# One key tile stacked from high and low parts, read once, with the queries in both halves; the rotation of two pairs of query tiles in the other order

## The chip, the cores and the metric

The kernel runs on one core of one Trainium2 chip. The metric is device time in microseconds (us) of one execution. TensorE (PE, with its weight loads PEld), VectorE (DVE), ScalarE (ACT) and GpSimd (POOL) compute; SyncE (SP) and ACT issue the transfers (DMAs) that are spoken of here. A file of instructions runs in order on each engine, and an instruction that waits holds up all behind it on its engine, the DMAs that the engine issues among them.

## The reference

One encoder layer on two batches with the same weights, T = 512 + 256 = 768 tokens of width D = 2048, in fp32:

```
h = rmsnorm(x);  z = h @ w_in        # columns: 1024 fourier | 1024 q | 256 k | 256 v
of = Re(fft2 over (tokens, 128 channels)) of each of 8 groups, times a 128x128 matrix each
q, k = rope(q), rope(k)              # 16 query heads, 4 key/value heads, head_dim 64
oa = softmax of q k^T / 8 within +-128 tokens, with a sink per head in the denominator, times v
x = x + concat(rmsnorm(of), rmsnorm(oa)) @ w_out
u = relu(rmsnorm(x) @ w_up);  x = x + (u*u) @ w_down;  y = rmsnorm(x)
```

## The kernel before

A value in fp32 is split into a high part, rounded to the fast fp32r format, and a low part, the remainder; a product of two such values is then three fp32r matmuls (high by high, high by low, low by high). For weights ACT makes the high part (`wh`, L69) and DVE the low part (`wl`, L70) of a `raw` tile loaded by SP (L79).

The phases are, in time: the values and the first products of the Fourier group (L268, L391), the in-projection together with the Fourier stages and the rotary step, the attention together with the out-projection (L1046, L1048), the MLP up (L1193) and the MLP down (L1628).

The in-projection (`pz`, L802) runs in 20 pieces of 48 matmuls, four pieces to a *pair*, which is 256 columns as two tiles of 128. Pair 0 is the keys, pairs 1 to 4 are queries; `order` gives the group g of heads that a pair feeds (pair 1 feeds g = 2, pair 2 g = 0, pair 3 g = 1, pair 4 g = 3). At the end of a pair ACT copies PSUM into a tile `zs` (L815), one COPY for each of two column tiles and two halves of the tokens. Pairs 0 and 1 go to DRAM and are read back later by SP (`load_z`, L678). Pairs 2 and 3 keep their `zs` in one buffer that they use in turn.

The rotary step of a pair goes over three slices of 256 tokens. For each slice POOL makes two products with the sine table (`cross`, `zy`, L687), DVE multiplies by the cosine (`turned`, L694) and adds or subtracts `zy` (L696), and `parts` makes the high part `zh` on ACT (L706 for keys, L709 for queries), writes it to DRAM from ACT's queue (`put`, L704), makes the low part on DVE (L707, L710) and writes that also. The tables of sine, cosine and mask are loaded by SP in `open_attention` (L664), and DVE scales two of them (L666). `zy` and `zh` have two buffers each.

What is done beside the matmuls is hung on the pieces by `after(piece, fn)`, half pieces included; this list sets the place of cross, turned and parts, of `load_z`, `load_k` (L719) and `load_q` (L730). TensorE's order is written out throughout; the order of the other engines comes from a scheduler up to piece 18 and is written out from piece 19 on. The pool `kp` holds mask, sine, cosine, keys, `zy`, `zh`, one `zs` and the query tiles `qs`.

In the attention there are 24 units (b, g): 128 query tokens and the four heads of group g, against up to 384 keys. A score tile takes two matmuls over 128 contraction rows, which are 64 head dimensions times two parts (`qk`, L848). Before, `qs` holds the high part of the queries in partitions 0 to 63 and the low part in 64 to 127, `kdh` holds the high part of the keys twice and `kdl` the low part twice, so that `qs` by `kdl` and `qs` by `kdh` add up all four products. Four loads of 64x3072 fill `kdh` and `kdl`; two loads fill `qs` of a unit, whose buffers are two.

## Time and profile before

| | us |
|---|---|
| median of three runs (2589.88, 2593.62, 2589.92) | 2589.92 |
| the profiled execution | 2589.64 |
| its span, first to last instruction | 2587.8 |
| in-projection: piece 11 ends / piece 15 ends | 311.4 / 344.91 |
| first score matmul | 378.9 |
| TensorE's last matmul ends | 2579.9 |

The mean granted TensorE clock is 0.999 of full speed. In the rows of the profile, times are us from the start of the span; in a row of the timeline stand start, duration, engine, line and operation with output and inputs, shape, number of instructions put together, and in brackets the idle time of the engine before it with what ended it. PEld is TensorE's loading of stationary operands, SPq and ACTq are the queues from which DMAs are issued.

## The change

Three things are changed. First, the keys' high and low parts are written to one DRAM tile of 512 rows and read by one load of 128x3072 into one tile `kd`, high part in partitions 0 to 63, low part in 64 to 127. Second, `qs` of a unit becomes twice as large: the high part in both halves of the partitions and the low part in both halves, four loads for two; the score is `kd` by the low queries plus `kd` by the high queries. Third, the rotary step of pair 1 moves in the list from 16.5 to 13.5 (its load from 12 to 11), ahead of pair 3's, which stays at 15. The load of the keys is one item at 15, those of the first two units' queries move from 18 and 18.5 to 17.5 and 18. The two `zs` in `kp` get two buffers, and `zh` takes a tile of the size of the new `qs`.

```diff
-    kr_d = [dpool.tile([2 * P, T], F32, tag=f"k{c}", name=f"k{c}") for c in "hl"]
+    kr_d = dpool.tile([4 * P, T], F32, tag="k", name="k")
...
-            for name in ("kdh", "kdl"):
-                kt[name] = kp.tile([P, NKV, T], F32R, tag=name, name=name)
+            kt["kd"] = kp.tile([P, NKV, T], F32R, tag="kd", name="kd")
...
-            zt[pair] = (zo["p"] if pair in (2, 3) else kt["kp"]).tile([P, 2, T], F32, tag="zs", name="zs")
+            zt[pair] = zo["p"].tile([P, 2, T], F32, tag="zs", name="zs") if pair in (2, 3) else kt["kp"].tile([P, 2, T], F32, tag="zs", name="zs", bufs=2)
...
-            out, scale = (kr_d, None) if pair == 0 else (qr_d[order[pair]], HD ** -0.5)
-            hi = kt["kp"].tile([P, 2, 256], F32R, tag="zy" if pair == len(cols) - 1 else "qs", name="zh", bufs=2)
+            out, scale = ([kr_d[o * 2 * P : (o + 1) * 2 * P] for o in range(2)], None) if pair == 0 else (qr_d[order[pair]], HD ** -0.5)
+            if pair == len(cols) - 1:
+                hi = kt["kp"].tile([P, 2, 256], F32R, tag="zy", name="zh", bufs=2)
+            else:
+                hi = kt["kp"].tile([P, 2, 4, P], F32R, tag="qs", name="zh", bufs=2)[:, 0].rearrange("p (b h) t -> p b (h t)", b=2)
...
-        def load_k(i):
-            h = slice(i % 2 * HD, (i % 2 + 1) * HD)
-            nc.sync.dma_start(f32(kt["kdh" if i < 2 else "kdl"][h]), kr_d[i // 2][:].rearrange("(d h) t -> d h t", h=NKV))
+        def load_k():
+            nc.sync.dma_start(f32(kt["kd"][:]), kr_d[:].rearrange("(p h) t -> p h t", h=NKV))
...
-            qs = kt["kp"].tile([P, 4, P], F32R, tag="qs", name="qs", bufs=2)
+            qs = kt["kp"].tile([P, 2, 4, P], F32R, tag="qs", name="qs", bufs=2)
             state[u] = {"qs": qs}
-            for o in range(2):
-                nc.sync.dma_start(f32(qs[o * HD : (o + 1) * HD]), qr_d[g][o][:, t0].rearrange("(d h) t -> d h t", h=4))
+            for i in range(2):
+                for o in range(2):
+                    nc.sync.dma_start(f32(qs[i * HD : (i + 1) * HD, o]), qr_d[g][o][:, t0].rearrange("(d h) t -> d h t", h=4))
...
-        for pair, t, ahead in ((0, 10.5, 10), (2, 11.5, None), (3, 15, None), (1, 16.5, 12)):
+        for pair, t, ahead in ((0, 10.5, 10), (2, 11.5, None), (1, 13.5, 11), (3, 15, None)):
...
-        for i in range(4):
-            after(14.5 + i, lambda i=i: load_k(i))
+        after(15, load_k)
         for u in range(2):
-            after(18 + 0.5 * u, lambda u=u: load_q(u))
+            after(17.5 + 0.5 * u, lambda u=u: load_q(u))
...
-            for n, kd in enumerate((kdl, kdh)):
-                nc.tensor.matmul(s[:, :nk], st["qs"][:, h, :], kd[:, g, k0 * P : k0 * P + nk], start=(n == 0), stop=(n == 1))
+            for o in range(2):
+                nc.tensor.matmul(s[:, :nk], st["qs"][:, 1 - o, h, :], kd[:, g, k0 * P : k0 * P + nk], start=(o == 0), stop=(o == 1))
```

On ACT, after the third slice of pair 2, before the change (`wh_3666` and `wh_3736` are weights of pair 4; `zs_3696` is the tile of pair 3; qh0 and ql0 are the DRAM tiles of group 0):

```order
L709 ACTIVATE zh_3583<-zs_3403 128x512
L704 DMA qh0_82<-zh_3583 128x2x256
L704 DMA ql0_83<-zs_3403 128x2x256
L69 ACTIVATE wh_3666<-raw_3554 128x4x4x64
L69 ACTIVATE wh_3736<-raw_3616 128x4x4x64
L815 COPY zs_3696<-pz_3457 128x384
L815 COPY zs_3696<-pz_3458 128x384
```

The same place on ACT after the change (line numbers move by one or two; `zs_3455` is the tile of pair 1, qh2 and ql2 the DRAM tiles of group 2, `zs_3719` the tile of pair 3, `wh_3689` and `wh_3767` the former `wh_3666` and `wh_3736`):

```order
L711 ACTIVATE zh_3673<-zs_3455 128x512
L69 ACTIVATE wh_3689<-raw_3552 128x4x4x64
L706 DMA qh2_85<-zh_3673 128x2x256
L706 DMA ql2_86<-zs_3455 128x2x256
L711 ACTIVATE zh_3681<-zs_3455 128x512
L706 DMA qh2_85<-zh_3681 128x2x256
L706 DMA ql2_86<-zs_3455 128x2x256
L711 ACTIVATE zh_3725<-zs_3455 128x512
L706 DMA qh2_85<-zh_3725 128x2x256
L706 DMA ql2_86<-zs_3455 128x2x256
L69 ACTIVATE wh_3767<-raw_3614 128x4x4x64
L816 COPY zs_3719<-pz_3457 128x384
```

The parts of pair 1 now stand ahead of the COPYs of pair 3; before they came behind them and behind pair 3's own parts.

On SP, from the load of pair 0's `zs` on, before the change:

```order
L678 DMA zs_3371<-zs0_78 128x2x768
L79 DMA raw_3465<-in_w_in 128x4x256
L79 DMA raw_3554<-in_w_in 128x4x256
L719 DMA kdh_3369<-kh_80 64x3072
L678 DMA zs_3548<-zs1_79 128x2x768
L79 DMA raw_3616<-in_w_in 128x4x256
L719 DMA kdh_3369<-kh_80 64x3072
L79 DMA raw_3670<-in_w_in 128x4x256
L719 DMA kdl_3370<-kl_81 64x3072
```

And after the change:

```order
L677 DMA zs_3369<-zs0_78 128x2x768
L677 DMA zs_3455<-zs1_79 128x2x768
L79 DMA raw_3465<-in_w_in 128x4x256
L79 DMA raw_3552<-in_w_in 128x4x256
L720 DMA kd_3368<-k_80 128x3072
L79 DMA raw_3614<-in_w_in 128x4x256
L79 DMA raw_3693<-in_w_in 128x4x256
```

The load of pair 1's `zs` moved up behind that of pair 0, and one load of the keys stands where four stood among the weights.

On DVE, after the last `wl` that stands ahead of pair 1's steps, after the change:

```order
L70 TENSOR_TENSOR wl_3611<-raw_3465,wh_3610 128x4x4x64
L693 TENSOR_TENSOR zs_3455<-zs_3455,cosr_3360 128x2x256 x2
L695 TENSOR_TENSOR zs_3455<-zs_3455,zy_3640 128x256
L712 SCALAR_TENSOR_TENSOR zs_3401<-zs_3401,zh_3581 128x2x256
L695 TENSOR_TENSOR zs_3455<-zs_3455,zy_3640 128x256
L695 TENSOR_TENSOR zs_3455<-zs_3455,zy_3643 128x256 x2
L693 TENSOR_TENSOR zs_3455<-zs_3455,cosr_3360 128x2x256
L712 SCALAR_TENSOR_TENSOR zs_3455<-zs_3455,zh_3673 128x2x256
L695 TENSOR_TENSOR zs_3455<-zs_3455,zy_3686 128x256 x2
L70 TENSOR_TENSOR wl_3690<-raw_3552,wh_3689 128x4x4x64
L712 SCALAR_TENSOR_TENSOR zs_3455<-zs_3455,zh_3681 128x2x256
```

Before the change `wl_3613` (now `wl_3611`) was followed by the low part of pair 2's last slice and by three `wl`.

More of the change, by code (lines that the diff above doesn't have):

```diff
@@ L832, in hybrid_encoder @@
     pp3 = att.enter_context(tc.tile_pool(name="pp3", bufs=1, space=PSUM, reuse_waits="tile"))
-    mask, sink, kdh, kdl = (kt[c] for c in ("mask", "sink", "kdh", "kdl"))
+    mask, sink, kd = (kt[c] for c in ("mask", "sink", "kd"))
     def key_blocks(b):
```

## The prediction

> **What bounds the kernel now.** I read the page first, then the waits of TensorE (its matmul stream PE and its weight loads PEld), and then the timeline of the one stretch that the change rewrites.

> ```profile
> PE 2575.5 (100%) x13580; PEld 2358.4 (91%) x13580; DVE 1812.4 (70%) x2222; ACT 1124.0 (43%) x1574; POOL 249.6 (10%) x353
> PE 94%; DVE 2%; DMA 1%; POOL 1%; ACT 0%; issue 0%; SPq 0%; ACTq 0%; POOLq 0%; DVEq 0%
> ```

> TensorE is busy 2575.5 of the span's 2587.8 us, and the chain that ended last is 94% PE. Nothing in the change removes a matmul: each score tile still takes two of the same shape. So the change can give at most what TensorE now waits for, and it can cost whatever new wait it brings. Two lists, of PE and of its weight loads, of which I show two rows each:

> ```profile
> PE pv L391 <- ACT wh L69: 1.1, 1, 1.1
> ...
> PE pz L802 <- ACT zs L815: 0.4, 1, 0.4
> ```

> ```profile
> PEld pu L1193 <- ACT o L1211: 1.3, 7, 0.2
> PEld pz L802 <- ACT zs L815: 0.9, 2, 0.7
> ```

> Columns are total us, times, longest. The first row of each pair is the largest of its list. Only `pz L802 <- ACT zs L815` lies in the stretch that is rewritten, and it is 0.4 us on PE (the weight loads run ahead of the matmuls, so theirs of 0.9 is mostly covered). That is the whole gain on offer there. A gain of over 0.2% (5.2 us, which is about what a measurement of this kernel can tell from no change) isn't there to be had. The question is what new waits cost. The place of that one wait, on the timeline:

> ```profile
> 344.40 0.51 PE L802 MATMUL pz<-xs,wl 128*128 128x384 f32 x2
> ...
> 344.80 0.86 ACT L815 COPY zs<-pz 128x384 f32<-128x384 f32 x2 [2.10 <-PE pz L802]
> ...
> 345.33 1.17 PE L802 MATMUL pz<-xf,wh 128*128 128x384 f32 x4 [0.42 <-ACT zs L815]
> ```

> Piece 15 ends on PE at 344.91; piece 16 needs a PSUM bank that ACT's first COPY of pair 3 empties, and starts at 345.33. There is no slack here: each us by which ACT reaches that COPY later is a us on the kernel.

> **The change, part by part.**

> *Earlier tables and earlier rotation (pairs 0 and 2).* The keys' tiles take less room in the pool, so its first tiles lie elsewhere; the order's waits show the load of the mask freed by the last matmul of the second Fourier stage instead of POOL's `ssf` sum.

> ```profile
> 297.35 0.28 PE L630 MATMUL pz<-tabh,al 128*128 128x256 f32 x1
> ...
> 299.78 1.84 POOL L641 TENSOR_TENSOR ssf<-ssf,sq 128x768 f32<-128x768 f32 x1
> ...
> 301.65 0.34 SPq L664 DMA_DIRECT2D mask<-in_c_mask  x1
> ...
> 303.48 0.43 SPq L678 DMA_DIRECT2D zs<-zs  x1
> ...
> 307.79 0.96 DVE L666 TENSOR_TENSOR sinr<-sinr,rb 128x768 f32<-128x768 f32 x1 [1.17 <-DMA sinr<-in_c_sin]
> ...
> 311.12 2.15 POOL L687 TENSOR_TENSOR zy<-zs,sinr 128x256 f32<-128x256 f32 x3 [6.31 <-DMA raw<-in_w_in]
> ```

> The mask may go at 297.35 + 0.28 = 297.63 instead of 301.65, so the loads behind it move up by about 4.0 us. POOL's first product at 311.12 then waits no longer for its load but for DVE's `sinr`, whose own 1.17 us of waiting goes: it ends near 307.79 - 1.17 + 0.96 = 307.6. So rotation starts 311.12 - 307.7 = 3.4 us earlier. By itself this is worth nothing: no PE wait hangs on it but the 0.42 above.

> *Pair 1's rotation moved ahead of pair 3's.* This is the part that counts. In order, ACT now has to do three `zh`, six puts and one `wh` more before it reaches `wh_3767` and the COPY of pair 3: three `zh_3673`, `zh_3681`, `zh_3725`, each with a put of its high and of its low part. The costs of one (min, median and max in ns; the last row is of this tile's loads and puts):

> ```profile
> L696 DVE TENSOR_TENSOR zs<-zs,zy x30: 409/420/987, 315.1 to 443.4; 128x256 f32<-128x256 f32 x30
> ...
> L709 ACT ACTIVATE zh<-zs x12: 615/632/634, 326.4 to 443.9; 128x512 fp32r<-128x512 f32 x12
> L710 DVE SCALAR_TENSOR_TENSOR zs<-zs,zh x12: 662/686/1226, 329.7 to 447.2; 128x512 fp32r<-128x512 f32 x12
> L704 ACTq DMA_DIRECT2D ql<-zs x12: 366/374/1027, 330.5 to 447.9; - x12
> ...
> DMA to landing us min/median/max: 2.1/2.5/4.8
> ```

> As bare work that is 3 x 0.63 + 6 x 0.37 = 4.1 us. ACT's spare time ahead of the COPY is 1.47 + 2.10 + 2.10 us in the rows below and above, so the work fits; the chain of waits inside it does not. ACT is in order, so each put waits for DVE's low part, and each third `zh` waits until the put of the one two before has landed, since there are two such buffers:

> ```profile
> 334.42 0.63 ACT L709 ACTIVATE zh<-zs 128x512 fp32r<-128x512 f32 x1 [4.26 <-DMA qh<-zh]
> ...
> 336.52 2.05 ACT L69 ACTIVATE wh<-raw 128x1024 fp32r<-128x1024 f32 x1 [1.47 <-PE pz L802]
> ...
> 340.67 2.03 ACT L69 ACTIVATE wh<-raw 128x1024 fp32r<-128x1024 f32 x1 [2.10 <-DMA raw<-in_w_in]
> ```

> ```profile
> 329.53 4.81 DMA qh<-zh
> ...
> 335.81 8.93 DMA ql<-zs
> ```

> The chain has a fixed anchor: the `wh` at 336.52 waited for PE to be done with a weight tile, so it can't go earlier after the change either (there it is `wh_3689`, and stands between `zh_3673` and its put). From there:
> - `wh_3689` ends at 336.52 + 2.05 = 338.57. The put of `zh_3673`'s high part goes then, and its low part's at 338.94, to 339.3.
> - `zh_3681` to 339.95, its put to 340.3. DVE does `wl_3690` from 338.6 (2.0 us) and then the low part (0.69) to 341.3; that put ends at 341.7.
> - `zh_3725` needs this, and the put of 338.57 landed. The page's only row for such a wait has 4.81 us for that landing, which gives 343.4. I take it, because it is the same transfer, with weights on the way.
> - Then in series `zh` 0.63, the low part 0.69, its put 0.37, `wh_3767` 2.05, one COPY (half of 0.86) 0.43 = 4.2, so that PE goes on at 347.6 instead of 345.33: **+2.3 us**.

> Bounds: if the put lands in 2.5 us (the median in that last row), 341.7 decides and the sum is 345.9: +0.6. If it takes 8.93 us, the longest put that the chain shows, it is 347.5 + 4.2 = 351.7: +6.4. Below +0.6 only the end of the 0.42 wait would do, and nothing shortens ACT's row of work, so I exclude it.

> The chain holds only if `zh_3673` is done by 336.5. Before, DVE's `wl` of 331.28 closed pair 2; 3.4 us earlier that is 327.9. Behind it DVE has two cosine products, two short steps and a low part ahead of `zh_3673`. And POOL now runs pair 1's six products beside them. What that does to both engines shows here:

> ```profile
> 321.46 3.52 POOL L687 TENSOR_TENSOR zy<-zs,sinr 128x256 f32<-128x256 f32 x2 [1.99 <-DVE zs L696]
> ...
> 321.81 2.58 DVE L70 TENSOR_TENSOR wl<-raw,wh 128x1024 fp32r<-128x1024 f32 x1
> ...
> 326.34 1.75 POOL L687 TENSOR_TENSOR zy<-zs,sinr 128x256 f32<-128x256 f32 x2 [1.36 <-DVE zs L696]
> ...
> 331.28 2.00 DVE L70 TENSOR_TENSOR wl<-raw,wh 128x1024 fp32r<-128x1024 f32 x1
> ```

> Alone a `wl` takes 2.00 us and two products 1.75; side by side 2.58 and 3.52. Counting 1.5 us of it for the end of pair 2 and each step of pair 1 at its slow price (2.58 + 2 x 1.2 + 2 x 0.4 + 0.69), `zh_3673` can start near 327.9 + 1.5 + 6.5 = 335.9, just in time for the anchor. So this race is open, and some 2 us more of it move the COPY by as much. [...]
